# A four-layer trunk on one core: the sliding-window layer starts one query tile earlier, ends its gate tiles at head 12, and takes the sink as a key

## The chip, the cores and the metric

The kernel runs on one core of a Trainium2 chip. A core has TensorE (PE in the profile, its weight loads PEld), VectorE (DVE), ScalarE (ACT), GpSimd (POOL) and SyncE (SP, which here only issues transfers). The metric is the device time of one execution in microseconds (us); the kernel is run several times and the median counts.

## The reference

A trunk of four layers on x of 512 x 1024 (float32). Each layer is x + RMSNorm(branch(RMSNorm(x))), and each branch has an input projection, a mixer, a SiLU gate and an output projection. The mixers are a state-space layer, sliding-window attention, latent attention and a gated MLP. The change is in the second, for which the reference computes, with 16 heads of 64, two k/v heads, and a window of 128:

```python
q, k, v, z = jnp.split(h @ w_in, [SWA_WIDTH, SWA_WIDTH + kv_w, SWA_WIDTH + 2 * kv_w], axis=-1)
...
s = jnp.einsum('bnqhgd,bnkhd->bnhgqk', qb, kb).astype(jnp.float32) * (HEAD_DIM ** -0.5)
...
s = jnp.where(valid[None, :, None, None], s + bias, NEG_INF)
sink = jnp.broadcast_to(sinks.astype(jnp.float32).reshape(SWA_KV_HEADS, grp, 1, 1), s.shape[:-1] + (1,))
p = jax.nn.softmax(jnp.concatenate([s, sink], axis=-1), axis=-1)[..., :-1]
o = jnp.einsum('bnhgqk,bnkhd->bnqhgd', p.astype(v.dtype), vb)
...
return (o * jax.nn.silu(z)) @ w_out
```

The sink is one more logit of each softmax, without a value.

## The kernel before

Every dense product is done with operands split into a high part (fp32r) and a low part, three matmuls for one: high x high, low x high, high x low. XH and XL hold the layer's normalised input, transposed, and later, in the same memory, the gated output of the mixer, which the output projection reads.

**Weights** go through a list of chunks of 1 MB (`add`, L208). A chunk is loaded by SP into one of two buffers (`wraw`), copied to its high part `wh` by ACT, and its low part `wl` is the difference, made by POOL in one instruction of 128 x 2048 (L160), or, for chunks marked "mix", in four pieces alternating between POOL and DVE. `wh` and `wl` have two buffers each, and a third is kept for chunks marked "x". `get` (L191) hands out the next chunk; `ahead(n)` (L199) issues the splits of the next n chunks and the load of the one behind.

**Order.** A planner orders the instructions of each engine by priority and by its own estimate of when their inputs are ready, so what is issued first in the code can run later. Instructions issued through `act_`, `dve_`, `pool_`, `pe_`, or passed to `after`, keep their program order. On the chip every engine then runs its list in order. PSUM has eight banks, and every product takes one (`bank`).

**The sliding-window layer** (`layer_b`, L1360) does its input projection in tiles of 128 output features by 512 tokens, 24 matmuls each. The first four tiles (k, v, and query tiles 0 and 1) are done in two halves of 256 tokens: `fm_first` does the first half during the output projection of the layer before, `fm_rest` (L1289) the second half and then the copy out of PSUM. The fourteen other tiles come one by one from `Dense.step` (L1303): query tiles 2 to 7 and gate tiles z0 to z7. A query tile holds two heads; `evac_q` (L1378) copies its high part by ACT and subtracts its low part by DVE. v is turned by four transposes as soon as it is there, and the scores of head 0 are issued behind query tile 0.

For each head `scores(h)` (L1419) makes four blocks of scores on PE; DVE adds the bias, writes P and takes the row maximum in one instruction per block (L1433); `nm` is minus the larger of maximum and sink (L1439); ACT takes the exponential with its row sum, four instructions (L1444), and the sink's exponential `es` (L1446). `normalise(h)` adds `es` to the sums, takes the reciprocal and scales P on DVE (L1455). `p_transposes(h)` transposes P on PE, with the copies out split between DVE (L1473) and ACT (L1471). `pv(hp)` multiplies with v for a pair of heads and gates the result into `zt` (L1487). P has two buffers, so the scores of a head need the transposes two heads back. The loop over heads (L1494) issues the normalisation of head h, the scores of head h + 1, a dense tile, every second time a `pv`, and the transposes of head h. The last two gate tiles are done in halves, in heads 12, 13 (two), and 14.

`act_split(hp)` (L1489) splits a gated pair of heads from `zt` into XH and XL: ACT copies (L226), POOL or DVE subtracts (L227). XH and XL are the inputs of the dense tiles, so this may be written only after the last of them.

**The output projection** (`out_proj`, L290) has four blocks of 128 tokens, two column halves and two chunks of weights for each. It begins with the first chunk for all four blocks (12 matmuls each, into four banks that stay open), needing head pairs 0 to 3; the rest of the layer (`tail`: `pv(7)` and `act_split(7)`) is issued between them. All four layers use it.

Of the kernel before, what the change touches and what calls it, by code (L numbers as in the profile page):

```python
# [10 lines left out]
F32 = mybir.dt.float32  # L11
# [36 lines left out]
def tile_hybrid_trunk(ctx: ExitStack, tc: tile.TileContext, I, out, depth=4):  # L48
# [241 lines left out]
    def out_proj(SH, SL, x, begin, tail, emit_x, nxt, first):  # L290
# [9 lines left out]
        def mms(bt, t, i, HL, last, ks=range(4)):  # L300
            H, L = HL
            for k in ks:
                st, en = (i == 0 and k == 0), (last and k == 3)
                sh, sl = SH[:, t, 4 * i + k, :], SL[:, t, 4 * i + k, :]
                pe_.matmul(bt[:], lhsT=sh, rhs=H[:, k, :], start=st, stop=False)
                pe_.matmul(bt[:], lhsT=sh, rhs=L[:, k, :], start=False, stop=False)
                pe_.matmul(bt[:], lhsT=sl, rhs=H[:, k, :], start=False, stop=en)
# [1052 lines left out]
    def layer_b(tiles, reload):  # L1360
# [5 lines left out]
        sp.dma_start(out=sink[:], in_=dram("b_sinks", 0, [[0, 128], [1, 16]]))  # L1366
        bias = b1.tile([128, 16, 256], F32, name="bias")
# [21 lines left out]
        def evac(i, bt):  # L1389
# [29 lines left out]
        def scores(h):  # L1419
            g, q = h // 8, qs[h // 2][:, h % 2]  # L1420
            P = b1.tile([128, 4, 256], F32, name="P", bufs=2)
            mx = sb_.tile([128, 4], F32, name="mx")
            for pr in range(2):
# [6 lines left out]
                for n in (2 * pr, 2 * pr + 1):  # L1430
# [63 lines left out]
        for h in range(16):  # L1494
# [9 lines left out]
            elif 0 < h < 15:  # L1504
                dense.step()
# [517 lines left out]
```

## Time and profile before

| | |
|---|---|
| median of three runs | 1047.23 us (1045.99, 1047.23, 1049.91) |
| the profiled execution | 1044.97 us |
| its span, first to last instruction | 1043.2 us |
| mean granted clock of TensorE | 0.97 |
| busy: PE, PEld, DVE, ACT, POOL | 967.5, 798.5, 677.3, 488.1, 423.2 us |
| the sliding-window layer | about 305 to 475 us, its output projection behind it |

The profile gives for each engine the time that it executes instructions. A share of the whole span is an average over stages, so the views used here are taken by stretch of time: the busy time in a stretch with PEclk, the clock that TensorE was granted (1.00 is full); groups of instructions with their number, busy time and mean duration (ns), and the idle time of the engine before them with what ended it; waits, as "engine tile line <- what released it: us in total, times, longest"; and the timeline, with start and duration in us. Matmuls are pipelined, so a matmul's duration is longer than its distance to the next. An arrow reads out <- in.

### The profile page before, as it was taken

How to read it: one execution, taken by the hardware profiler on the slowest of the kernel's cores; microseconds unless marked ns; L12 is line 12 of the kernel's file. 1: busy time of each engine (PE TensorE's matmuls, PEld its weight loads, DVE VectorE, ACT ScalarE, POOL GpSimd, SP SyncE). 2: the span in 40 equal slices, each digit the busy share in tenths (PEclk: the TensorE clock that was granted, in tenths of full speed). 3: DMA queues.
4: the chain of work that ended last, by engine and by line, in shares of the span. 5: the costliest groups of instructions: out<-in, count | busy, mean ns of one | idle time of the engine just before them, and what ended most of it. 6: DMA issues, size and time to landing. Idle time of an engine off the chain costs nothing.

```text
span 1043.2 us, 14407 instructions
## 1 busy us (share of the span) xinstructions
PE 967.5 (93%) x5343; PEld 798.5 (77%) x5343; DVE 677.3 (65%) x1536; ACT 488.1 (47%) x1082; POOL 423.2 (41%) x325
## 2 busy tenths in 40 slices
PE   7879989999987999969899999999979999999997
PEld 6768988778777778757797877777747778888785
DVE  7998887735766867776840335878884876514454
ACT  4557776543456465562553252354463553322221
POOL 6775774666232122333436341312063433431210
PEclk8979999999998999989999999999999999999999
DMA  9211211454254132115034422110225032233011
GB/s 237 74 38 41 82 42 41 173 121 141 86 153 126 41 122 81 41 41 161 1 112 127 121 63 68 46 46 4 79 81 178 27 119 83 84 118 106 26 66 65
DMA packets 69223, 90.40 MB, mean 87 GB/s; under 512 B 13592, under 2 KB 49312, under 8 KB 69024
## 3 DMA queue, kind: packets, MB, share of 16 engines
q1 hardware_dynamic: 66944, 80.76, 25.2%
q10 hardware_dynamic: 2208, 8.72, 2.3%
q8 instruction: 42, 0.69, 0.3%
q14 instruction: 29, 0.24, 0.1%
HBM read 83.44 MB, written 4.98 MB: 85 GB/s over the span
## 4 chain that ended last, share of the span: by engine, by line
PE 62%; DVE 22%; ACT 9%; issue 4%; POOL 2%; DMA 0%; ACTq 0%; DVEq 0%; SPq 0%; POOLq 0%
PE bank L66 22%; PE bank L218 6%; PE bank L217 6%; PE bank L216 6%; PE bank L1792 4%; PE bank L1793 4%; PE bank L1794 4%; PE bank L101 2%; DVE rs_t L66 2%; DVE rs_y L66 2%; ACT P L1444 2%; PE bank L1685 2%; DVE xt L66 1%; PE bank L1729 1%; DVE P L1455 1%
## 5 line engine op out<-in xcount | busy, mean ns | idle before, releaser
L160 POOL TENSOR_TENSOR wl<-wraw,wh 128x2048 fp32r<-128x2048 f32 (+3 forms) x37 | 138.5, 3750 | 264.0 <-ACT wh L156 263.2
L217 PE MATMUL bank<-XL,wh 128*128 128x512 f32 (+1 forms) x542 | 186.9, 345 | 7.7 <-DVE XL L66 7.0
L216 PE MATMUL bank<-XH,wh 128*128 128x512 f32 (+1 forms) x542 | 188.6, 349 | 0.1
L218 PE MATMUL bank<-XH,wl 128*128 128x512 f32 (+1 forms) x542 | 186.6, 345 | 1.9 <-POOL wl L160 1.8
L66 POOL TENSOR_TENSOR wl<-wraw,wh 128x512 fp32r<-128x512 f32 (+1 forms) x63 | 90.1, 1454 | 104.0 <-ACT wh L66 90.5
L217 PEld LDWEIGHTS bank<-XL,wh 128*128 128x128 f32 x542 | 104.7, 193 | 20.6 <-DVE XL L66 7.7
L218 PEld LDWEIGHTS bank<-XH,wl 128*128 128x128 f32 x542 | 104.5, 193 | 14.7 <-POOL wl L160 2.2
L216 PEld LDWEIGHTS bank<-XH,wh 128*128 128x128 f32 x542 | 104.6, 193 | 12.6 <-ACT XH L1614 0.5
L66 PE MATMUL bank<-wh,XH 128*128 128x512 f32 (+1 forms) x320 | 112.6, 365 | 0.9 <-ACT g L66 0.9
L66 PE MATMUL bank<-wh,XL 128*128 128x512 f32 (+1 forms) x320 | 109.6, 355 | 0.0
L66 PE MATMUL bank<-wl,XH 128*128 128x512 f32 (+1 forms) x320 | 109.6, 355 | 0.0
L156 ACT CAST wh<-wraw 128x2048 fp32r<-128x2048 f32 (+3 forms) x50 | 71.0, 1439 | 45.8 <-PE bank L217 21.0
L1793 PE MATMUL bank<-wl,XH 128*128 128x512 f32 x192 | 76.3, 397 | 3.8 <-DVE wl L66 3.8
L66 DVE TENSOR_TENSOR wl<-wraw,wh 128x512 fp32r<-128x512 f32 x42 | 57.4, 1395 | 32.8 <-ACT wh L66 30.9
L1792 PE MATMUL bank<-wh,XH 128*128 128x512 f32 x192 | 76.8, 400 | 0.0
L1794 PE MATMUL bank<-wh,XL 128*128 128x512 f32 x192 | 76.3, 397 | 0.0
L66 PEld LDWEIGHTS bank<-wh,XH 128*128 128x128 f32 x320 | 60.3, 194 | 9.7 <-ACT g L66 1.1
L66 PEld LDWEIGHTS bank<-wh,XL 128*128 128x128 f32 x320 | 59.9, 193 | 9.1 <-DVE XL L66 0.2
L66 ACT CAST wh<-wraw 128x512 fp32r<-128x512 f32 (+1 forms) x105 | 59.4, 636 | 15.0 <-DMA wraw<-in_a_w_out_dram 7.6
L66 PEld LDWEIGHTS bank<-wl,XH 128*128 128x128 f32 x320 | 60.1, 194 | 8.2
L1694 ACT ACTIVATE P<-P,nm 128x512 f32<-128x512 f32 (+1 forms) x64 | 35.2, 550 | 53.4 <-DVE nm L1691 53.4
L1444 ACT ACTIVATE P<-P,nm 128x128 f32<-128x128 f32 (+1 forms) x64 | 30.1, 471 | 61.6 <-DVE nm L1439 61.6
(362 smaller groups left out, 2100.0 us busy)
## 6 DMA issues: line engine op xcount, KB each, us to landing
wraw<-in_d_w_in_dram SPq DMA_DIRECT2D x12, 1024.0 KB, 5.1
wraw<-in_b_w_in_dram SPq DMA_DIRECT2D x9, 1024.0 KB, 5.2
wraw<-in_c_w_in_dram SPq DMA_DIRECT2D x8, 1024.0 KB, 7.7
wraw<-in_a_w_in_dram SPq DMA_DIRECT2D x7, 1024.0 KB, 5.3
wraw<-in_c_w_uq_dram SPq DMA_DIRECT2D x8, 576.0 KB, 4.7
wraw<-in_a_w_glu_dram SPq DMA_DIRECT2D x4, 1024.0 KB, 5.1
wraw<-in_a_w_out_dram SPq DMA_DIRECT2D x4, 1024.0 KB, 5.0
wraw<-in_b_w_out_dram SPq DMA_DIRECT2D x4, 1024.0 KB, 4.9
```

The source lines that it names most:

```text
L66: return lambda *a, **k: after(f(*a, **k))
L101: pe.matmul(out_ap, lhsT=in_ap, rhs=ident[0:k, 0:k], is_transpose=True, start=True, stop=True)
L156: (act_ if c["eng"] in MIX else act).copy(h, r)
L160: es[(i + k) % len(es)].tensor_tensor(out=l, in0=r, in1=h.bitcast(F32), op=SUB)
L216: pe.matmul(out_ap, lhsT=lh, rhs=rh, start=(i == 0), stop=False)
L217: pe.matmul(out_ap, lhsT=lh, rhs=rl, start=False, stop=False)
L218: pe.matmul(out_ap, lhsT=ll, rhs=rh, start=False, stop=(i == n - 1))
L1444: act.activation(out=P[:, n, k0:256], in_=P[:, n, k0:256], func=AF.Exp, bias=nm[:, n:n + 1], accum_out=sums[:, n:n + 1])
L1694: act.activation(out=P[n][:], in_=P[n][:], func=AF.Exp, scale=scale, bias=nm[:, n:n + 1], accum_out=sums[:, n:n + 1])
L1792: pe.matmul(bt[:], lhsT=xh, rhs=H[:, k, :], start=(i == 0 and k == 0), stop=False)
L1793: pe.matmul(bt[:], lhsT=xh, rhs=L[:, k, :], start=False, stop=False)
L1794: pe.matmul(bt[:], lhsT=xl, rhs=H[:, k, :], start=False, stop=(i == 1 and k == 3))
```

## The change

Five things:

1. `layer_b` calls `ahead(1)` before `fm_rest`, so the split of the third weight chunk (query tiles 2 and 3) is issued ahead of the four first tiles.
2. The turning of v is a function of its own (`turn_v`). After `fm_rest` come one dense tile (query tile 2), then the turning of v, then the scores of head 0. All other dense tiles move up by one head, and the last, z7, is done whole in head 12; no tile is done in halves.
3. The sink becomes a 257th column of P. The scores are written negated, so DVE's reduction is a minimum that starts from minus the sink (a pointer scalar in place of a constant) and yields `nm` directly; ACT copies the sink's column into P (four elements a partition) and its exponentials run over 257 columns with scale -1. `nm`'s own instruction, `es` and the addition of `es` are gone.
4. The first chunk of the output projection is a class, `OutFirst`, of which `layer_b` calls `step` in heads 13, 14 and 15 (blocks 0, 1 and 2). `out_proj` does what steps are left: one in this layer, all four in the others, whose order stays the same.
5. The splits into XH and XL of head pairs 0 to 5 are issued in head 12 and of pair 6 in head 14, where before pairs 0 to 6 were issued in head 15. Pairs 0 to 3 and 7 are subtracted by DVE, 4 to 6 by POOL (before, odd pairs by DVE and even by POOL). In head 15 `ahead(2)` takes the place of `ahead(1)`, and `OutFirst` asks for one chunk ahead in this layer where `out_proj` asked for two. `tail` begins with `pv(7)`, behind all of the first chunk.

```diff
+    def out_mms(SH, SL, bt, t, i, HL, last, ks=range(4)):
...
+    class OutFirst:
+        def __init__(self, SH, SL, first):
+            self.S, self.first, self.bts = (SH, SL), first, []
+
+        def step(self):
+            t = len(self.bts)
+            if t == 0:
+                self.c0 = get()
+                ahead(self.first)
+            self.bts.append(bank())
+            out_mms(*self.S, self.bts[t], t, 0, self.c0, False)
+
-    def out_proj(SH, SL, x, begin, tail, emit_x, nxt, first):
+    def out_proj(pre, x, begin, tail, emit_x, nxt):
...
-        c0 = get()
-        ahead(first)
-        bts = []
-        for t in range(4):
-            bts.append(bank())
-            mms(bts[t], t, 0, c0, False)
+        while len(pre.bts) < 4:
+            pre.step()
             next(tail, None)
+        bts = pre.bts
...
+        nsink = b1.tile([128, 16], F32, name="nsink")
+        act.mul(nsink[:], sink[:], -1.0)
...
             elif i == 1:
                 act.copy(perm_out(vT[:]), perm_in(bt))
-                b2 = bank()
-                for n in range(4):
-                    transpose(b2[:, 128 * n:128 * n + 128], vT[:, 128 * n:128 * n + 128])
-                dve.tensor_copy(vs[:], b2[:].rearrange("p (n d) -> p n d", n=4))
             else:
                 evac_q(i - 2, bt)
-                if i == 2:
-                    scores(0)
+
+        def turn_v():
...
-            P = b1.tile([128, 4, 256], F32, name="P", bufs=2)
-            mx = sb_.tile([128, 4], F32, name="mx")
+            P = b1.tile([128, 4, 260], F32, name="P", bufs=2)
+            nm = sb_.tile([128, 4], F32, name="nm")
+            act.copy(P[:, :, 256:257], bc(bc(nsink[:, h:h + 1], 1, 4)[:, :, 0], 2, 1))
...
-                        out=P[:, n, k0:256], in0=sb[:, o0:o0 + 256 - k0], in1=bias[:, h, k0:256], scale=0.125,
-                        scalar=-3e38, op0=ADD, op1=MAX, accum_out=mx[:, n:n + 1])
+                        out=P[:, n, k0:256], in0=sb[:, o0:o0 + 256 - k0], in1=bias[:, h, k0:256], scale=-0.125,
+                        scalar=nsink[:, h:h + 1], op0=ADD, op1=ALU.min, accum_out=nm[:, n:n + 1])
...
-            nm = sb_.tile([128, 4], F32, name="nm")
-            dve.tensor_scalar(out=nm[:], in0=mx[:], scalar1=sink[:, h:h + 1], scalar2=-1.0, op0=MAX, op1=MUL)
             sums = sb_.tile([128, 4], F32, name="sums")
-            es = sb_.tile([128, 4], F32, name="es")
             for n in range(4):
                 k0 = 0 if n else 128
-                act.activation(out=P[:, n, k0:256], in_=P[:, n, k0:256], func=AF.Exp, bias=nm[:, n:n + 1],
+                act.activation(out=P[:, n, k0:257], in_=P[:, n, k0:257], func=AF.Exp, scale=-1.0, bias=nm[:, n:n + 1],
                                accum_out=sums[:, n:n + 1])
-            act.activation(out=es[:], in_=nm[:], func=AF.Exp, bias=sink[:, h:h + 1])
...
-            dve.tensor_tensor(out=sums[:], in0=sums[:], in1=es[:], op=ADD)
...
-                       dve if hp % 2 else pool)
-
+                       dve if hp < 4 or hp == 7 else pool)
+
+        ahead(1)
         fm_rest(tiles, evac)
+        dense.step()
+        turn_v()
+        scores(0)
         for h in range(16):
...
-            if h in (12, 13, 14):
-                for _ in range(2 if h == 13 else 1):
-                    dense.half()
-            elif 0 < h < 15:
+            if 0 < h < 13:
                 dense.step()
+            elif h >= 13:
+                pre.step()
             if h and h % 2 == 0:
                 pv(h // 2 - 1)
             if h == 6:
                 reload()
+            if h == 12:
+                for hp in range(6):
+                    act_split(hp)
+            if h == 14:
+                act_split(6)
             if h == 15:
-                ahead(1)
-                for hp in range(7):
-                    act_split(hp)
+                ahead(2)
             p_transposes(h)
 
         def tail():
-            yield
             pv(7)
             act_split(7)
+            B.close()
             yield
-            B.close()
         return tail()
```

More of the change, by code (lines that the diff above doesn't have):

```diff
@@ L288, in transpose_block @@
         x_low(bvs, t)
-    def out_proj(SH, SL, x, begin, tail, emit_x, nxt, first):
+    def out_mms(SH, SL, bt, t, i, HL, last, ks=range(4)):
+        H, L = HL
+        for k in ks:
+            st, en = (i == 0 and k == 0), (last and k == 3)
+            sh, sl = SH[:, t, 4 * i + k, :], SL[:, t, 4 * i + k, :]
+            pe_.matmul(bt[:], lhsT=sh, rhs=H[:, k, :], start=st, stop=False)
+            pe_.matmul(bt[:], lhsT=sh, rhs=L[:, k, :], start=False, stop=False)
+            pe_.matmul(bt[:], lhsT=sl, rhs=H[:, k, :], start=False, stop=en)
+    class OutFirst:
[9 more added lines that the diff above has]
+    def out_proj(pre, x, begin, tail, emit_x, nxt):
         ssq = [sm.tile([128, 2], F32, name="ssq") for t in range(4)]
@@ L298, in cs, with mms @@
             return slice(512 * n, 512 * n + 512)
[L300 to L307, printed above, removed]
+        def mms(*a):
+            out_mms(*pre.S, *a)
         def junk():
@@ L1358, in bias_lines, with layer_b @@
         sp.dma_start(out=scr, in_=bc(line[:], 1, 32))
-    def layer_b(tiles, reload):
+    def layer_b(tiles, pre, reload):
         B = ExitStack()
@@ L1399, in evac @@
                 act.copy(perm_out(vT[:]), perm_in(bt))
-                b2 = bank()
-                for n in range(4):
-                    transpose(b2[:, 128 * n:128 * n + 128], vT[:, 128 * n:128 * n + 128])
-                dve.tensor_copy(vs[:], b2[:].rearrange("p (n d) -> p n d", n=4))
             else:
                 evac_q(i - 2, bt)
-                if i == 2:
-                    scores(0)
+        def turn_v():
+            b2 = bank()
+            for n in range(4):
+                transpose(b2[:, 128 * n:128 * n + 128], vT[:, 128 * n:128 * n + 128])
+            dve.tensor_copy(vs[:], b2[:].rearrange("p (n d) -> p n d", n=4))
         def z_evac(kk):
@@ L1433, in scores @@
                     i = dve.tensor_tensor_reduce(
[L1434 to L1435 removed]
+                        out=P[:, n, k0:256], in0=sb[:, o0:o0 + 256 - k0], in1=bias[:, h, k0:256], scale=-0.125,
+                        scalar=nsink[:, h:h + 1], op0=ADD, op1=ALU.min, accum_out=nm[:, n:n + 1])
                     if h == 1:
                         after(i)
[L1438 to L1439 removed]
             sums = sb_.tile([128, 4], F32, name="sums")
[L1441 removed]
             for n in range(4):
                 k0 = 0 if n else 128
[L1444 removed]
+                act.activation(out=P[:, n, k0:257], in_=P[:, n, k0:257], func=AF.Exp, scale=-1.0, bias=nm[:, n:n + 1],
                                accum_out=sums[:, n:n + 1])
[L1446 to L1447 removed]
+            Ps[h], nms[h] = P, sums
         def normalise(h):
[L1450 to L1451 removed]
+            P, sums = Ps[h], nms.pop(h)
             dve.reciprocal(out=sums[:], in_=sums[:])
@@ L1509, in layer_b, with layer_c @@
                 reload()
+            if h == 12:
[3 more added lines that the diff above has]
+                act_split(6)
             if h == 15:
-                ahead(1)
-                for hp in range(7):
-                    act_split(hp)
+                ahead(2)
             p_transposes(h)
         def tail():
-            yield
             pv(7)
             act_split(7)
+            B.close()
             yield
-            B.close()
         return tail()
-    def layer_c(tiles, open_right, close):
+    def layer_c(tiles, pre, open_right, close):
         Cx = ExitStack()
@@ L1940, in tile_hybrid_trunk @@
     tail = iter(())
+    pre = OutFirst(YH, YL, 2)
     for l in range(depth):
@@ L1968, in tile_hybrid_trunk @@
             break
+        pre = OutFirst(XH, XL, 2 if l == 2 else 1)
         if l == 0:
-            tail = layer_b(tiles, lambda: after(sp.dma_start(
+            tail = layer_b(tiles, pre, lambda: after(sp.dma_start(
                 out=xt[:], in_=xd.rearrange("(b p) d -> p b d", p=128))))
@@ L1982, in close @@
                     right["loads"] = d_loads(pl)
-            tail = layer_c(tiles, open_right, close)
+            tail = layer_c(tiles, pre, open_right, close)
         else:
```

4 lines of the change are left out of this document (1 added, 3 removed).

## The prediction

> **What bounds the kernel now.** I read the page first, then the busy time by stretch around the sliding-window layer (it runs from about 305 to 481 us), then the waits of TensorE there, then the timeline at the two places where TensorE waits.
>
> ```profile
> span 1043.2 us, 14407 instructions
> ...
> PE 967.5 (93%) x5343; PEld 798.5 (77%) x5343; DVE 677.3 (65%) x1536; ACT 488.1 (47%) x1082; POOL 423.2 (41%) x325
> ```
>
> TensorE is busy 93% of the span, so time is to be had only where PE stands still or runs slow.
>
> ```profile
> core 0: us, PE busy (x) PEld busy (x) DVE busy (x) ACT busy (x) POOL busy (x), PEclk, DMA share, GB/s
> 306.30:347.70 41.40, 33.95 (x214) 30.72 (x212) 26.26 (x56) 24.77 (x48) 7.13 (x3) 0.92 0.43 102
> 347.70:434.20 86.50, 83.94 (x470) 67.01 (x469) 61.45 (x174) 47.80 (x112) 22.97 (x5) 1.00 0.25 86
> 434.20:480.90 46.70, 37.77 (x248) 31.18 (x247) 33.25 (x75) 23.28 (x58) 18.03 (x8) 0.93 0.23 70
> ```
>
> ```profile
> 319.00:323.00 4.00, 4.00 (x23) 4.00 (x23) 3.92 (x4) 3.61 (x4) 3.20 (x3) 0.58 0.03 7
> 329.00:333.00 4.00, 4.00 (x15) 3.33 (x14) 2.15 (x10) 1.75 (x7) 0.00 (x0) 0.57 1.01 340
> 457.00:462.00 5.00, 2.94 (x22) 1.93 (x22) 3.00 (x14) 3.46 (x12) 0.00 (x0) 1.00 0.00 0
> 466.00:470.00 4.00, 3.85 (x13) 3.29 (x14) 4.00 (x4) 2.90 (x6) 3.59 (x1) 0.61 0.01 4
> ```
>
> The middle of the layer (347.7 to 434.2) leaves PE idle 2.6 us of 86.5. The start leaves 41.40 - 33.95 = 7.45 us. The end, from the scores of head 13 to the last matmul of the output projection's first chunk, leaves 46.70 - 37.77 = 8.93 us. Both also have stretches of slow clock: 4 us at 0.58 and 4 us at 0.57 cost 1.7 us each against full speed, 3.85 busy us at 0.61 cost 1.5. So the start loses 7.45 + 3.4 = 10.9 us, the end 8.93 + 1.5 = 10.4 us, together 21.3.
>
> Who makes PE wait, first for 306 to 348, then for 434 to 481:
>
> ```profile
> PE bank L1428 <- DVE qS L1386: 3.6, 1, 3.6
> PE bank L101 <- issue: 2.1, 1, 2.1
> PE bank L101 <- DVE P L1455: 1.8, 1, 1.8
> ```
>
> ```profile
> PE bank L101 <- DVE P L1455: 5.5, 3, 3.0
> PE bank L1484 <- DVE PT L1473: 3.5, 2, 2.8
> ```
>
> At the start the scores of head 0 (L1428) wait 3.6 us for the low half of their query tile, and the transposes of v 2.1 us for the copy of v. At the end transposes of P wait for the normalised P (5.5) and P.V for the copied transposes (3.5).
>
> ```profile
> 321.67 4.57 POOL L160 TENSOR_TENSOR wl<-wraw,wh 128x2048 fp32r<-128x2048 f32 x1 [0.80 <-POOL wl L66]
> ```
>
> ```profile
> 322.01 5.38 DVE L66 TENSOR_TENSOR wl<-wraw,wh 128x512 fp32r<-128x512 f32 x2
> 327.43 2.17 DVE L1386 TENSOR_TENSOR qS<-bank,qS 64x512 fp32r<-64x512 f32 x2
> ```
>
> This is why the query tile is late: two weight splits on DVE (L66) start while POOL splits the next chunk, last 5.38 us together until POOL is done, and the query's subtraction queues behind them.
>
> **The change, part by part.** Tiles first: the chain has 140 wide matmuls in 31.86 us, 0.228 each, so a dense tile of 24 is 5.5 us and 12 matmuls of the output projection 2.7. Narrow ones follow each other at 0.12.
>
> ```profile
> 475.38 31.86 PE bank L66 x140
> ```
>
> ```profile
> 306.56 0.12 PE bank L216
> ```
>
> ```profile
> L1396 DVE TENSOR_TENSOR kL<-bank,kH 64x512 fp32r<-64x512 f32 x4 | 4.5, 1113 | 8.9 <-ACT kH L1393 8.9
> ```
>
> ```profile
> L1393 ACT CAST kH<-bank 64x512 fp32r<-64x512 f32 x4 | 4.3, 1082 | 3.7 <-PE bank L218 3.6
> ```
>
> 1. *The split of the third chunk moves ahead of the first four tiles.* Its four copies on ACT and four subtractions (two DVE, two POOL) move from behind k and v to before them; the load of a later chunk, which needs that raw buffer, moves with them past the bias loads on SP. ACT sits idle 3.6 us before the k copies and DVE 8.9 before k's low half; four copies of 0.62 and two subtractions of 0.68 undisturbed fit in. Cost nothing; if that cover were gone, about 2.5 us on the path k copies, k low, scores.
>
> 2. *One query tile before v is turned and before the first scores.* PE gets 5.5 us of work whose only input is step 1. The order of work becomes: k, v, q0, q1 (narrow, 24 x 0.12 = 2.8 each), the q tile, v turned, scores of head 0. One narrow tile still runs before k, so the q tile starts at about 306.5 + 5 x 2.8 = 320.5 and ends at 326. Without the weight splits in its way, the k chain takes its 4.3 (ACT) + 4.5 (DVE) from 312.3, the end of k's tile, to about 321, query tile 0 follows with 2.2 to about 323.5: 2.5 us before PE asks. The third wait (1.8) goes too, as head 0 is normalised behind a whole dense tile. What is late next is that 2.5 us margin, so I leave 1 us and take 10.9 - 1 = 9.9 us.
>
>    The trace says what a gap costs in clock: 2.1 us of waiting at 318 was followed by 4 us at 0.58, while the 2.8 us before 457 left 457 to 462 at 1.00. The Trainium skill, "TensorE: Matmul & The Clock Gate", Part 1, lets the clock fall after at least one idle window of about 3.4 us; by it the first gap would cost no clock and the start would be worth 1.7 us less. The 0.58 row contradicts it here, so I keep the row.
>
> 3. *The sink as a key.* Each head loses `nm` (L1439), the exponential `es` and the addition of `es`; it gains a 4-column copy on ACT. The score reductions take a pointer scalar instead of a constant.
>
> ```profile
> L1439 DVE TENSOR_SCALAR nm<-mx,sink x16: 224/230/2106, 331.0 to 458.3; 128x4 f32<-128x4 f32 x16
> L1446 ACT ACTIVATE es<-nm,sink x16: 281/282/285, 333.1 to 460.4; 128x4 f32<-128x4 f32 x16
> ```
>
> ```profile
> L66 DVE SCALAR_TENSOR_TENSOR zt<-zt,y x6: 677/678/1053, 202.0 to 205.4; 128x512 f32<-128x512 f32 x6
> L66 DVE SCALAR_TENSOR_TENSOR zt<-zt,rs_y,gpre x4: 744/748/751, 8.6 to 22.7; 128x512 f32<-128x512 f32 x4
> ```
>
>    Out of each head's loop go 0.23 (up to 2.1 where `nm` waited out POOL), 0.2 and 0.16. The new copy is bounded by the `es` row above (0.28, where its issue slot costs as much) and by zero, since it can run while ACT waits; I take it as equal to `es`. The pointer scalar's price on this reduction isn't in the trace: nearest is 748 against 678 ns, pointer against constant in another DVE form, +0.07; below is zero. Four per head make 0 to 0.28, I take 0.28. Net about 0.3 us off a loop that in the middle is covered by dense matmuls: worth 0 there, 2.6 at most (its idle time).
>
> 4. *z tiles end at head 12, the output projection's first 36 matmuls in heads 13 to 15.* PE's work is the same: one more dense tile early, 2.7 us in each of heads 13, 14, 15 instead of 2.7, 5.5 (head 13), 2.7, 0 from head 12 on. What they need is XH and XL of head pairs 0 to 3, which may be written only after z7's matmuls.
>
> ```profile
> L226 ACT CAST XH<-zt 128x512 fp32r<-128x512 f32 x8 | 4.6, 619 | 6.2 <-DVE zt L1487 6.2
> ```
>
> ```profile
> L227 DVE TENSOR_TENSOR XL<-zt,XH 128x512 fp32r<-128x512 f32 x4 | 7.1, 1786 | 0.7 <-ACT XH L226 0.7
> L1455 DVE TENSOR_SCALAR P<-P,sums 128x256 f32<-128x256 f32 x12 | 6.0, 555 | 0.0
> L1433 DVE CUSTOM_DVE_ANT_0 P<-bank,bias 128x256 f32<-128x256 f32 x12 | 4.5, 418 | 0.0
> ```
>
> ```profile
> DVE sums L1451 <- ACT es L1446: 8.3, 4, 2.2
> ```
>
> ```profile
> 473.72 1.67 PE bank L1484 x16
> ```
>
>    Behind z7 PE still has P.V (1.67), transposes (about 0.8) and scores (8 x 0.12 = 0.95): 3.4 us, against ACT's first copy at 0.62, each next one 0.62 later, and DVE's subtraction 0.68 behind it: four pairs by about 3.2. The projection's first matmuls just find them, if ACT takes the copies at once.
>    Then each head is a loop: exponentials 2.2 (the wait of L1451), reciprocal and normalisation about 1.5, copy of transposes 0.7, reductions 1.5: 5.9 us. PE's share per head is 2.7 + 0.95 + 0.8 + half of 1.67 = 5.3. So the loop is about 0.6 longer for three heads, 1.8 us, and the last transposes stand uncovered for about 1.2. DVE's extra four subtractions (2.7 us) fit in its 2.2 us waits per head, but POOL's 4.6 us split of the projection's second chunk now falls into heads 13 and 14 and can hold up a normalisation: 1.5. Residue 4.5; gain 10.4 - 4.5 = 5.9 us.
>
> 5. *Head pair 7 comes last.* P.V of pair 7 now follows the whole first chunk, where before 24 matmuls (5.5 us) came behind it.
>
> ```profile
> 475.43 0.69 DVE L1487 SCALAR_TENSOR_TENSOR zt<-bank,zt 128x512 f32<-128x512 f32 x1
> 476.81 0.69 DVE L227 TENSOR_TENSOR XL<-zt,XH 128x512 fp32r<-128x512 f32 x1 [0.69 <-ACT XH L226]
> ```
>
>    From the gate at 475.43, with ACT's copy (0.62) between, to the end of the subtraction at 477.50 it takes 2.1 us. The new cover is nine matmuls on pairs 4 to 6, 2.05 us, and two more on XH: cost 0 to 0.5, I take 0.5. The load of the post-norm gain starts at that event too and is now wanted after one tile instead of two; only DVE's gain multiply waits for it, and PE's next need of DVE is two column blocks later.
>
> Sum: 9.9 + 5.9 - 0.5 = 15.3 us. The profiled execution took 1044.97 (span 1043.2 and 1.8 around it), 2.3 below the median of the runs, 1047.23. So 1029.7 in the profiled execution's terms, 1032 against the median, which is the forecast.
>
> **Rivals.**
>
> *The end's hole only moves* (1037). The four subtractions at head 12 or a normalisation meet POOL, and the projection's matmuls stand at the head of PE's queue with transposes 13 and scores 15 behind them.
>
> ```profile
> 466.28 5.69 DVE L227 TENSOR_TENSOR XL<-zt,XH 128x512 fp32r<-128x512 f32 x2
> ```
>
> ```profile
> 466.41 5.01 POOL L160 TENSOR_TENSOR wl<-wraw,wh 128x2048 fp32r<-128x2048 f32 x1 [0.47 <-ACT wh L156]
> ```
>
> For it: two subtractions that take 0.69 alone took 5.69 beside POOL's 5.01. One such meeting costs 4.3 us, and a slow clock behind it 1.5: the end's 5.9 is gone, 1047.2 - 9.9 = 1037. The Trainium skill, "SBUF — State Buffer", SBUF: two separate sides, makes it a rule: the port pair shared by both is locked for a whole instruction; the trace agrees. Against: POOL's splits of pairs 4 and 5 come behind ACT's copies of 0 to 3. Chance 0.20.
>
> *The start comes out as before* (1041): the order of unpinned work is the planner's. For it: the trace has matmuls of q0 in front of v's transposes, which the code issues first.
>
> ```profile
> 315.50 0.28 PE L218 MATMUL bank<-XH,wl 128*128 128x256 f32 x1
> 317.86 0.63 PE L101 MATMUL bank<-ident,vT 128*128 128x128 f32 x4 [2.08 <-issue]
> ```
>
> If it pulls the next chunk's 4.6 us split in front of the query's subtraction, the wait of 3.6 stays, and with it the clock. Then only the end's gain is left, 5.9 or so. Chance 0.13.
>
> *Slower: DVE becomes the bound of each head* through the reduction with the pointer. In the middle DVE is busy 61.45 of 86.5 us over about ten heads: 2.5 us of slack per head, 0.6 for each of the four reductions. From 0.42 + 0.6 = 1.0 us on each head grows; it takes 0.25 more each (x 64 = 16 us) to eat the gain, so 1.3 us is the point. At 1.5 the kernel ends near 1032 + 64 x 0.5 = 1064. Nothing in the trace comes near: +0.07. Chance 0.07.
>
> *No difference*: both holes return elsewhere, at 1046. Chance 0.08.
>
> **How the numbers follow.** The forecast itself has the remaining 0.52, at 1032. The low end takes all 21.3 us of both ends and the 2.6 of the middle: 1047.2 - 23.9 = 1023. The high end takes in the first two rivals, to 1042. A measurement of this kernel tells about 0.5%, 5 us, from no change. Faster: 0.52 + 0.20 and two thirds of 0.13, 0.80; same: the rest of that and no difference, 0.13; slower 0.07.
>
> **What would show it.** Right: no wait of the first scores on the query's low half, clock 1.00 from 306 to 347, v's transposes behind a wide tile; the layer's matmuls of the output projection starting between the scores of heads 14 and 15; reductions at 0.42 to 0.50 us. Wrong: a wait of the projection's first matmul on XL, subtractions of 2 to 5 us at head 12, PE gaps over 2 us in heads 13 to 15, or the third chunk's split still behind the k copies.

## The result, and the profile after

The changed kernel took 1018.38 us (median of 1017.59 to 1019.33), the kernel before 1046.68 in the same comparison: a ratio of 0.9724, 95% interval 0.9701 to 0.9747. That is 28.3 us less, where 15.3 had been forecast, and below the low end of 1023. The profiled execution has a span of 1015.6 us. Times here and below leave out a few executions in a slower state, far above the others of the same kernel.

```profile
span 1015.6 us, 14293 instructions
...
PE 956.1 (94%) x5295; PEld 788.3 (78%) x5295; DVE 661.3 (65%) x1505; ACT 488.6 (48%) x1083; POOL 422.2 (42%) x324
```

The stretch of the layer, from the transposes of the last block before it to the end of the projection's first chunk with P.V of pair 7, by busy time: first before, then after.

```profile
306.56:480.90 174.34, 155.40 (x925) 128.65 (x924) 120.95 (x303) 95.60 (x217) 48.12 (x16) 0.96 0.29 86
```

```profile
307.84:454.80 146.96, 146.13 (x878) 121.21 (x876) 102.44 (x270) 95.79 (x217) 47.16 (x15) 1.00 0.31 95
```

It is 27.4 us shorter, nearly the whole gain. PE's idle time fell from 18.94 to 0.83 us, its clock from 0.96 to 1.00, and its *busy* time fell by 9.3 us for the same products. About 5 us of that is the slow clock, which the prediction had counted (3.4 + 1.5); the other 4 us or so were not traced. What PE still waits for between 305 and 456 us:

```profile
PE bank L101 <- DVE P L1469: 0.8, 1, 0.8
PE bank L66 <- ACT hblk L66: 0.6, 1, 0.6
```

In the chain of the last three heads the blocks of the output projection's first chunk (L66 x12) stand between transposes and scores, with no wait among them:

```profile
436.94 2.80 PE bank L66 x12
439.73 0.76 PE bank L101 x7
441.44 2.77 PE bank L66 x12
...
446.80 2.78 PE bank L66 x12
...
453.15 1.67 PE bank L1498 x16
```

The groups show one more thing: the idle time of ACT ahead of the exponentials, before (L1444) and after (L1460), fell from 61.6 to 27.1 us. It was the first sign that the key did more than had been forecast; it is not a measure of the gain, as the runs below show.

```profile
L1444 ACT ACTIVATE P<-P,nm 128x128 f32<-128x128 f32 (+1 forms) x64 | 30.1, 471 | 61.6 <-DVE nm L1439 61.6
```

```profile
L1460 ACT ACTIVATE P<-P,nm 128x129 f32<-128x129 f32 (+1 forms) x64 | 30.2, 475 | 27.1 <-DVE nm L1452 27.0
```

### The profile page after: what moved, and what is told of

It is laid out like the page before. It is cut to its first block, busy times and chain, and to the rows that moved or that the text cites. A ratio compares the mean times of both kernels' runs of the same rounds, so it can differ in the third digit from the quotient of the medians.

```text
span 1015.6 us, 14293 instructions
## 1 busy us (share of the span) xinstructions
PE 956.1 (94%) x5295; PEld 788.3 (78%) x5295; DVE 661.3 (65%) x1505; ACT 488.6 (48%) x1083; POOL 422.2 (42%) x324
## 4 chain that ended last, share of the span: by engine, by line
PE 68%; DVE 19%; ACT 5%; issue 4%; POOL 3%; DMA 0%; ACTq 0%; DVEq 0%; SPq 0%; POOLq 0%
PE bank L66 21%; PE bank L218 8%; PE bank L217 8%; PE bank L216 8%; PE bank L1811 4%; PE bank L1813 4%; PE bank L1812 4%; PE bank L101 3%; DVE rs_t L66 2%; DVE rs_y L66 2%; DVE xt L66 2%; PE bank L1704 2%; PE bank L1748 1%; PE bank L1498 1%; DVE P L1721 1%
## 5 line engine op out<-in xcount | busy, mean ns | idle before, releaser
L217 PE MATMUL bank<-XL,wh 128*128 128x512 f32 (+1 forms) x526 | 182.8, 347 | 7.7 <-DVE XL L66 7.0
L216 PE MATMUL bank<-XH,wh 128*128 128x512 f32 (+1 forms) x526 | 184.4, 352 | 0.1
L218 PE MATMUL bank<-XH,wl 128*128 128x512 f32 (+1 forms) x526 | 182.4, 347 | 1.8 <-POOL wl L160 1.8
L66 POOL TENSOR_TENSOR wl<-wraw,wh 128x512 fp32r<-128x512 f32 (+1 forms) x63 | 90.2, 1455 | 95.0 <-ACT wh L66 84.3
L217 PEld LDWEIGHTS bank<-XL,wh 128*128 128x128 f32 x526 | 100.5, 191 | 21.0 <-DVE XL L66 7.7
L218 PEld LDWEIGHTS bank<-XH,wl 128*128 128x128 f32 x526 | 100.4, 191 | 15.3 <-POOL wl L160 2.2
L66 PE MATMUL bank<-wh,XH 128*128 128x512 f32 (+1 forms) x320 | 111.2, 360 | 0.9 <-ACT g L66 0.9
L216 PEld LDWEIGHTS bank<-XH,wh 128*128 128x128 f32 x526 | 100.4, 191 | 13.1 <-ACT XH L1633 0.5
L66 PE MATMUL bank<-wl,XH 128*128 128x512 f32 (+1 forms) x320 | 108.8, 352 | 0.0
L66 PE MATMUL bank<-wh,XL 128*128 128x512 f32 (+1 forms) x320 | 108.5, 351 | 0.0
L66 DVE TENSOR_TENSOR wl<-wraw,wh 128x512 fp32r<-128x512 f32 x42 | 56.1, 1366 | 34.1 <-ACT wh L66 32.3
L66 PEld LDWEIGHTS bank<-wh,XH 128*128 128x128 f32 x320 | 59.1, 190 | 9.4 <-ACT g L66 1.1
L66 PEld LDWEIGHTS bank<-wh,XL 128*128 128x128 f32 x320 | 58.7, 189 | 9.0 <-DVE XL L66 0.2
L66 PEld LDWEIGHTS bank<-wl,XH 128*128 128x128 f32 x320 | 59.3, 191 | 8.0
L66 ACT CAST wh<-wraw 128x512 fp32r<-128x512 f32 (+1 forms) x105 | 59.4, 636 | 10.8 <-DMA wraw<-in_a_w_out_dram 7.9
L66 POOL TENSOR_TENSOR hblk<-xt,gpre 128x512 f32<-128x512 f32 x24 | 31.1, 1296 | 65.3 <-DVE xt L66 47.3
```

The costliest lines, as they stand in the source:

```text
L66: return lambda *a, **k: after(f(*a, **k))
L216: pe.matmul(out_ap, lhsT=lh, rhs=rh, start=(i == 0), stop=False)
L217: pe.matmul(out_ap, lhsT=lh, rhs=rl, start=False, stop=False)
L218: pe.matmul(out_ap, lhsT=ll, rhs=rh, start=False, stop=(i == n - 1))
```

## The experiments

**All combinations of three edits.** The change was taken apart into *start* (third chunk's split first, one query tile ahead of v's transposes and the first scores), *key* (sink as a key) and *end* (z tiles to head 12, first chunk in heads 13 to 15, its splits). Each was undone by putting the old lines back; where the counts of tiles did not fit, these lines differ from both kernels:

```diff
 # end without start: the fourteenth tile
-            if 0 < h < 13:
-                dense.step()
+            if 0 < h < 13:
+                for _ in range(2 if h == 12 else 1):
+                    dense.step()
 # start without end: thirteen tiles in the loop, z7 in halves
+            if h in (13, 14):
+                dense.half()
+            elif 0 < h < 12:
+                dense.step()
```

Start and end, without the key:

> The changed kernel with the old softmax (nm, es and the addition back, constant scalar in the reductions): start and end edits only. As predicted (the sink as a key is worth 0 in the middle, about 0.3 us a head in the last three): the changed kernel's 1018.4 plus 0 to 1, so 1018 to 1019.5. Rival, the key carries the middle: without it the 4.7 us that the middle gained beyond the forecast come back, 1023, PE waits on P L1469-like normalises or on nm between 345 and 434 us. Rival, the key also carries the end's surplus (7 us over 5.9 - 0.5): up to 1030.

Key and end, without the start:

> The changed kernel with the old start (v turned and scores 0 inside the first tiles, split of the third chunk behind them; the fourteenth dense tile runs at head 12 instead). As predicted: the start's 9.9 us come back and nothing else, 1028.3, with PE waits of about 3.6 on qS and 2.1 at the transposes of v. Rival, one tile more ahead of head 0 also carries the middle (DVE and ACT get a lead that lasts): 9.9 + 4.7, 1033.

Start and key, without the end:

> The changed kernel with the old end: 13 dense tiles are left for the heads, z6 whole at head 11, z7 as halves at heads 13 and 14, the four split pairs and the projection's first chunk behind head 15 as before. The tile that the start took comes out of the end, so its hole grows by up to 5.5 us: 1046.7 - 9.9 + 5.5 = 1042 if the end can't fill it, 1037 if the rest of the end is as before. If the key carries the middle: 4.7 less, 1033 to 1038.

The key alone:

> The kernel before with the sink as a key alone. As predicted: 0 in the middle and at most 2.6, 1044 to 1047; reductions 0.06 longer. Rival, the key shortens a loop that bounded the heads: 4.7 us in the middle and 2 in the last heads, 1040.

The end alone and the start alone, run later:

> The kernel before with the end edit alone (z tiles end at head 12, two of them there; out projection's first chunk in heads 13 to 15; head pair 7 last). My steps 4 and 5: 5.9 - 0.5 = 5.4 us less, 1042. If the head loop with the old softmax bounds the last heads (8 us lost there with start and end edits together): 1044 to 1047.

> The kernel before with the start edit alone (one query tile ahead of v's transposes and of the first scores; 13 dense tiles left, so the end has one half of z7 at heads 13 and 14 each). My step 2: 9.9 us less at the start, and up to 5.5 lost at the end, which has a tile less: 1037 to 1043. By the run with start and end edits (only 1.4 us gained at the start with the old softmax): no gain, 1044 to 1050.

Measured, with three distances read in the trace of one execution of each kernel: from the first copy of k (ACT, `kH`) to P.V of head pair 0 on PE; from there to P.V of pair 4; from there to the issue of the next layer's `rope` load. Where the start edit is in, one dense tile (5.5 us) has moved from the third stretch to the first; the table takes it out of the first and adds it to the third.

| edits | us | ratio to before, 95% | start | middle | end |
|---|---|---|---|---|---|
| none | 1046.7 | 1 | 42.1 | 68.8 | 109.8 |
| start | 1041.1 | 0.9929, 0.9912 to 0.9946 | 40.7 | 65.7 | 109.0 |
| end | 1040.2 | 0.9928, 0.9915 to 0.9941 | 41.7 | 68.8 | 103.7 |
| start, end | 1036.6 | 0.9891, 0.9878 to 0.9905 | 40.7 | 65.7 | 103.4 |
| key | 1032.2 | 0.9847, 0.9834 to 0.9860 | 39.9 | 67.4 | 95.8 |
| key, end | 1029.0 | 0.9817, 0.9801 to 0.9832 | 39.8 | 67.4 | 95.5 |
| start, key | 1024.1 | 0.9771, 0.9757 to 0.9784 | 31.4 | 65.6 | 99.2 |
| all (the change) | 1018.4 | 0.9724, 0.9701 to 0.9747 | 31.6 | 65.6 | 95.5 |

Here and below, differences are taken between ratios, times 1046.7, since each comparison had its own runs of the kernel before (by this measure the change gains 28.9). The key, which was priced at nothing, is the largest of the three: 16.0 us alone, 17.5 on top of the other two (0.9891 - 0.9724). All that was expected of the run without it (at most 1030), of the key alone (1040 at best) and of start and key (1033 at best) missed that. The run without the start came as expected, 1029.0 for 1028.3, with PE waiting 3.5 us for the query's low half and 2.0 before v's transposes. Alone the key shortens the end by 14.0 us; the end edit then adds 0.3, or 3.7 once the start has taken a tile away. The end edit alone gives 6.1 there. The start edit alone gains 1.4 at the start; on top of key and end, which have 2.3 there without it, it gains 8.2 more. The 1041 of the start edit alone falls in the range that step 2 gave, but by the middle, where the lead of one tile is worth 3.2.

**Why the key pays at the end.** DVE and ACT in one head, the kernel before:

```profile
448.77 0.28 DVE L1433 CUSTOM_DVE_ANT_0 P<-bank,bias 128x128 f32<-128x128 f32 x1
...
450.14 0.23 DVE L1439 TENSOR_SCALAR nm<-mx,sink 128x4 f32<-128x4 f32 x1
452.79 0.18 DVE L1452 RECIPROCAL sums<-sums 128x4 f32<-128x4 f32 x1
```

```profile
450.40 0.40 ACT L1444 ACTIVATE P<-P,nm 128x128 f32<-128x128 f32 x1 [3.89 <-DVE nm L1439]
```

and with the key alone:

```profile
438.95 0.33 DVE L1452 CUSTOM_DVE_ANT_0 P<-bank,bias,nsink 128x128 f32<-128x128 f32 x1
...
441.39 0.18 DVE L1466 RECIPROCAL sums<-sums 128x4 f32<-128x4 f32 x1 [0.89 <-ACT P L1460]
```

```profile
439.38 0.41 ACT L1460 ACTIVATE P<-P,nm 128x129 f32<-128x129 f32 x1 [1.11 <-DVE nm L1452]
```

Before, the first exponential starts 1.63 us after the first reduction: all four wait for one `nm` behind the fourth. With the key each waits for its own reduction, and the first starts after 0.43 us. From the first reduction to the reciprocal it takes 452.79 - 448.77 = 4.02 us before and 2.44 with the key: 1.2 less by the wait, 0.4 by the missing `es` and addition.

With the key alone PE waits for nothing from 434 to 482 us and its clock there is 1.00; before, it waited 5.5 + 3.5 us and ran at 0.53 and 0.61 from 462 to 470. The last two heads' normalisations also moved relative to POOL: before, three scalings took 1.80 us at 454.59 and 2.46 at 463.90, each beside POOL's subtractions (0.87 for three at 447.99, with POOL idle); with the key four take 1.08, at 441.61 and 449.07. How the 14.0 us split between the shorter wait and these meetings was not tested on the old end.

Two edits test the wait on the new one. One gives the change its wait back without an added instruction: the sink's column is written from all four minima.

```diff
-            act.copy(P[:, :, 256:257], bc(bc(nsink[:, h:h + 1], 1, 4)[:, :, 0], 2, 1))
 # behind the four reductions:
+            act.activation(out=P[:, :, 256:257], in_=nm[:].unsqueeze(2), func=AF.Identity, scale=0.0,
+                           bias=nsink[:, h:h + 1])
```

> The changed kernel with one edit: ACT's 4-column copy of the sink is written as 0 x nm + sink, so that it reads the row minima of all four blocks and stands ahead of the four exponentials. No instruction is added (the copy stays one ACT instruction of four columns). Theory A (the sink as a key pays because each block's exponential starts after its own reduction, while nm made all four wait for all four): most of what the old softmax cost comes back, 1018.4 plus 10 to 15, so 1028 to 1034, ACT waiting before each head's first exponential for the fourth reduction and PE for normalised P again. Rival B (it pays by the operations it removes, nm, es and the addition): 1018 to 1020, as all of them stay away.

Measured: 1023.5, ratio 0.9768 (0.9755 to 0.9780), 4.6 us more than the change: between A and B. A profile of it:

> The kernel with the restored wait (the sink's column written from all four minima) once more, for its trace: P.V of the first pair 37 us behind the first k copy as in the changed kernel (the start does not hang on the wait), and the 5 us that it lost in heads 13 to 15, where PE waits for normalised P.

P.V of pair 0 came 38.4 us behind the first k copy (37.1 in the change; the table has this less 5.5), and from P.V of pair 5 to that of pair 7 it took 23.4 us for 19.8: 1.3 lost at the start, 3.6 at the end. ACT's idle time ahead of the group is 42.2 us here. The other edit takes the wait out of the old softmax:

```diff
+                    dve.tensor_scalar(out=nm[:, n:n + 1], in0=mx[:, n:n + 1], scalar1=sink[:, h:h + 1], scalar2=-1.0,
+                                      op0=MAX, op1=MUL)
-            dve.tensor_scalar(out=nm[:], in0=mx[:], scalar1=sink[:, h:h + 1], scalar2=-1.0, op0=MAX, op1=MUL)
```

> Start and end edits with the old softmax (1036.6 when it ran), but nm computed for each block of its own, right behind that block's reduction: four DVE operations of one column for one of four. es and the addition stay. Theory A: the wait of all four exponentials for all four reductions is gone, so most of 17 us is gained, less 16 x (3 x 0.22 of nm, 0.2 of es, 0.17 of the addition) where DVE bounds a head: 1020 to 1026. Rival B: 48 more operations and none less: 1037 to 1042.

Measured: 1032.4, ratio 0.9850 (0.9833 to 0.9866), 4.3 less than with the old `nm`, with 48 operations more. P.V of pair 5 to pair 7 went from 27.8 to 23.1, the start only from 46.2 to 45.8. So the wait is worth 4 to 5 us, most of it in the last heads: theory A was right in kind and far too large. ACT's idle time ahead of the exponentials does not follow the time: it is 34.0 us here at 1032.4 and 26.5 with the key alone at 1032.2, against 27.1 in the change at 1018.4.

**Why the key pays at the start.** Start and end edits with the old softmax, PE's waits from 318 to 360 us and the busy time of ten of these:

```profile
PE bank L101 <- DVE P L1470: 6.9, 2, 5.7
```

```profile
337.00:347.00 10.00, 4.27 (x20) 3.34 (x19) 9.15 (x24) 5.05 (x12) 4.50 (x1) 0.79 0.16 42
```

DVE and POOL there:

```profile
335.93 0.81 DVE L1470 TENSOR_SCALAR P<-P,sums 128x128 f32<-128x128 f32 x3
337.70 2.19 DVE L1401 TENSOR_TENSOR qS<-bank,qS 64x512 fp32r<-64x512 f32 x2 [0.96 <-ACT qS L1398]
...
341.15 3.17 DVE L1470 TENSOR_SCALAR P<-P,sums 128x256 f32<-128x256 f32 x1
```

```profile
339.67 4.50 POOL L160 TENSOR_TENSOR wl<-wraw,wh 128x2048 fp32r<-128x2048 f32 x1 [15.29 <-ACT wh L156]
```

Three blocks of head 0 are normalised; the fourth is planned behind the query's subtraction and the next head's reductions, and lasts 3.17 us for some 0.3, until POOL's split ends (339.67 + 4.50 = 344.17). PE waits 5.7 us and then runs slow. In the change all four of head 0 go in one piece, ahead of POOL (head 1's four then take 2.30 us beside it, and PE waits the 0.8 shown above):

```profile
334.75 1.07 DVE L1469 TENSOR_SCALAR P<-P,sums 128x128 f32<-128x128 f32 x4
336.87 2.20 DVE L1403 TENSOR_TENSOR qS<-bank,qS 64x512 fp32r<-64x512 f32 x2 [1.05 <-ACT qS L1400]
```

The next edits keep that order with the old softmax, without and with `nm` by block:

```diff
             if h == 0:
+                normalise(0)          # its four scalings kept in program order
                 dense.step()
                 scores(1)
-            normalise(h)
+            else:
+                normalise(h)
```

> Start and end edits with the old softmax (1036.6), with head 0's normalisation written ahead of the next query tile and kept in that order: no operation is added or taken away. Without it DVE runs the fourth block of that normalisation behind the query's subtraction, where it meets POOL's split of a weight chunk and lasts 3.2 us for 0.29; PE waits 5.7 us and runs slow after it. Theory A2 (about 9 of the key's 17 us are this order at the start, the rest the end's loop): 1027 to 1029, P.V of the first pair 37 to 38 us behind the first k copy for 46.2. Rival (the start is lost by the length of the old softmax itself): 1034 to 1037.

> Both edits on the old softmax: head 0's normalisation kept ahead of the next query tile, and nm by block, so that each exponential follows its own reduction; es, the addition and four nm operations a head stay. Theory A2: the two gains add (9 at the start, 4 at the end), 1036.6 - 13 = 1023.5, the distance of some 4 to 5 to the changed kernel being the price of the operations that stay. If the operations cost nothing: 1019. If the order at the start is lost again: 1032.

The order alone gave 1032.7, ratio 0.9857 (0.9838 to 0.9877): 3.6 less, not 9. Its trace says why: head 0 is no longer late, but head 1's `nm` now meets POOL and lasts 2.56 us for 0.23, until POOL's end (339.58 + 4.61 = 344.19):

```profile
341.66 2.56 DVE L1454 TENSOR_SCALAR nm<-mx,sink 128x4 f32<-128x4 f32 x1
```

```profile
339.58 4.61 POOL L160 TENSOR_TENSOR wl<-wraw,wh 128x2048 fp32r<-128x2048 f32 x1 [15.34 <-ACT wh L156]
```

Both edits together gave 1022.3, ratio 0.9767 (0.9743 to 0.9790): 13.0 less, where the two alone gave 3.6 and 4.3. P.V of pair 0 now comes 38.6 us behind the first k copy, for 46.2 with neither, 44.2 with the order and 45.8 with `nm` by block. The second edit does two things, though. It also makes `nm` one column wide, and beside POOL's split these operations are not held, as head 1's of four columns was:

```profile
341.55 0.21 DVE L1454 TENSOR_SCALAR nm<-mx,sink 128x1 f32<-128x1 f32 x1
```

```profile
339.80 4.63 POOL L160 TENSOR_TENSOR wl<-wraw,wh 128x2048 fp32r<-128x2048 f32 x1 [14.62 <-ACT wh L156]
```

None of the 64 took more than 0.24 us. That fits a gain larger than the sum of the two, and it means that `nm` by block does not measure the joint wait alone; the edit on the sink's column does. So 13.0 of the key's 17.5 us are had without a sink column, by taking away ways in which a small operation is late.

**What the removed operations cost.** `es` and an addition put back into the change:

```diff
+            act.activation(out=es[:], in_=nm[:], func=AF.Exp, bias=sink[:, h:h + 1])
...
+            dve.scalar_tensor_tensor(out=sums[:], in0=es[:], scalar=0.0, in1=sums[:], op0=MUL, op1=ADD)
```

> The changed kernel with two operations of the old softmax put back where they hold up nothing but what they follow: the exponential es on ACT behind the four exponentials, and one DVE operation of four columns that adds 0 x es to the sums ahead of the reciprocal; no nm, each exponential still follows its own reduction. Predicted by my step 3 (0.2 + 0.16 us a head, covered in the middle): 1018.4 to 1019.5. Theory now (the 4 us between the old softmax with both waits broken, 1022.3, and the change are these operations): 1021 to 1023.

Both expectations missed: 1031.1, ratio 0.9842 (0.9830 to 0.9855), 12.4 us for some 0.36 us of operations a head. The start had the late fourth block again, and in head 13 three scalings, about 0.3 us each where POOL is idle, lasted 6.25 beside it, while ACT's idle time ahead of the exponentials was 26.3 us, no more than in the change:

```profile
340.93 2.92 DVE L1472 TENSOR_SCALAR P<-P,sums 128x256 f32<-128x256 f32 x1
...
438.74 6.25 DVE L1472 TENSOR_SCALAR P<-P,sums 128x256 f32<-128x256 f32 x3
```

```profile
438.43 1.54 POOL L227 TENSOR_TENSOR XL<-zt,XH 128x512 fp32r<-128x512 f32 x1 [10.11 <-ACT XH L226]
440.23 4.62 POOL L160 TENSOR_TENSOR wl<-wraw,wh 128x2048 fp32r<-128x2048 f32 x1 [0.27 <-ACT wh L156]
```

So the last test takes nothing away but the length of POOL's instruction: the layer's chunks are split in four pieces.

```diff
-                pool.tensor_tensor(out=l, in0=r, in1=h.bitcast(F32), op=SUB)
+            for i in range(4):
+                k = slice(i * n, i * n + n)
+                pool.tensor_tensor(out=l[:, k], in0=r[:, k], in1=h[:, k].bitcast(F32), op=SUB)
```

> The changed kernel with es and the addition put back (1031.1), with the same four pieces on POOL. There normalisations beside POOL's one instruction last 2.9 at the start and 6.3 us in head 13. Theory (the 12.7 us that two small operations cost are such meetings): most comes back, 1021 to 1025. Rival (the operations themselves, or the order): 1030 to 1032.

> Start and end edits with the old softmax (1036.6), but POOL makes the low half of this layer's weight chunks (input projection, and the first ones of the output projection) in four instructions of 128 x 512 for one of 128 x 2048: the same work, in pieces that end every 1.2 us. DVE's order at the start stays (the fourth block of head 0's normalisation behind the query's subtraction and a head's reductions). Theory (the start's loss is DVE shut out until POOL's instruction ends): the normalisation that lasted 3.2 lasts at most 1.5, PE's wait of 5.7 falls to some 4, and the last heads' meetings shrink too: 1029 to 1034. Rival (the loss is the order alone, or the length of the old softmax): 1035.5 to 1038.

With `es` and the addition: 1023.0, ratio 0.9748 (0.9728 to 0.9768): 9.8 of the 12.4 us came back, and the rest is within the intervals. The change itself was not run with the four pieces, so part of the 9.8 could be a gain that it would have too; the two groups above did get shorter, in the same places:

```profile
341.52 0.90 DVE L1480 TENSOR_SCALAR P<-P,sums 128x256 f32<-128x256 f32 x1
...
435.98 2.94 DVE L1480 TENSOR_SCALAR P<-P,sums 128x256 f32<-128x256 f32 x3
```

With the old softmax: 1035.2, ratio 0.9874 (0.9852 to 0.9895), no measurable gain over 0.9891, nearest its rival. The fourth block there lasted 1.16 us for 3.17, but `nm` behind it took 1.23 and PE still waited 3.7: the split into pieces makes each meeting shorter there, but not the order right. That the rest is the longer loop of the next head is likely and was not shown.

**The engine of the low halves**, the prediction's rival:

```diff
-                       dve if hp < 4 or hp == 7 else pool)
+                       dve if hp % 2 else pool)
```

> The changed kernel with the old choice of engine for the low halves: pairs 1, 3, 5 and 7 on DVE, 0, 2, 4 and 6 on POOL (in the change 0 to 3 and 7 on DVE). The rival of the prediction, one meeting of DVE and POOL on the shared port: a DVE normalisation or subtraction of 0.3 to 0.7 us lasts up to 4 or 5, and with the slow clock behind it the time rises by 4 to 6, 1022 to 1024. If the heads have that much slack: 1018 to 1019.5.

> The kernel with pairs 0 and 2 on POOL and 1 and 3 on DVE once more, for its trace: which operation of DVE beside POOL's subtractions or its chunk split lasts longer than alone in heads 12 to 15, and where PE waits for the 5 us that it lost.

Measured: 1023.7, ratio 0.9763 (0.9748 to 0.9778), some 4 us more than the change, the size that was expected, though its interval only just clears the change's and one execution took 1020.7. Its later profiled execution took 1019.4, with a layer 1.7 us longer (194.3 for 192.6 from the first k copy to the `rope` load) and a wait of 1.0 before a P.V. Whether a meeting cost the 4 us in the other executions stays open.

**The same idea in layer C.** Its causal attention has the same `nm`, and in the changed kernel it lasts up to 3.47 us, until POOL's end at 749.13:

```profile
745.69 3.47 DVE L1710 TENSOR_SCALAR nm<-mx 128x4 f32<-128x4 f32 x1
```

```profile
744.62 4.51 POOL L160 TENSOR_TENSOR wl<-wraw,wh 128x2048 fp32r<-128x2048 f32 x1
```

```diff
-  ... scale=1.0, scalar=-3e38, op0=ADD, op1=MAX, accum_out=mx[:, n:n + 1])
-            dve.tensor_scalar(out=nm[:], in0=mx[:], scalar1=-scale, scalar2=None, op0=MUL)
+  ... scale=-scale, scalar=3e38, op0=ADD, op1=ALU.min, accum_out=nm[:, n:n + 1])
-  ... func=AF.Exp, scale=scale, bias=nm[:, n:n + 1],
+  ... func=AF.Exp, scale=-1.0, bias=nm[:, n:n + 1],
```

> The changed kernel, with the same idea in layer C's causal attention: its reductions take scale -1/sqrt(96), minimum in place of maximum and write nm themselves, so the nm operation (L1710) goes and each block's exponential waits for its own reduction alone. Theory A: of layer C's PE waits on normalised P (7.3 us in the changed kernel) and of the slow clock after them (0.91 over 20 us, 0.88 over 28: 5 us) most goes: 1007 to 1012. Rival B: 16 operations of 0.2 to 0.3 us in a stage where PE has other work: 1015 to 1018.

Measured: 1007.8, ratio 0.9623 (0.9610 to 0.9635), 10.6 us less than the change and the fastest kernel of this study. PE's waits in layer C's heads, in the change and then without `nm`:

```profile
PE bank L101 <- DVE P L1721: 7.3, 7, 2.2
PE bank L218 <- POOL wl L160: 1.8, 2, 1.5
```

```profile
PE bank L101 <- DVE P L1719: 3.0, 3, 1.1
PE bank L1704 <- DVE nm L1707: 0.8, 1, 0.8
```

Beginning the projection's first chunk in layer C as well did not help:

```diff
+            if h >= 13:
+                pre.step()
-  ... zt[:, hp, :].rearrange("p (j c) -> p j c", j=4), pool)
+  ... zt[:, hp, :].rearrange("p (j c) -> p j c", j=4), dve if hp < 4 else pool)
```

> The changed kernel with layer C's nm gone (1007.8), and with the out projection's first chunk also begun in layer C: its blocks 0 and 1 in heads 13 and 14, low halves of pairs 0 to 3 on DVE in place of POOL. PE waits 1.1 + 0.8 us and runs at 0.91 for 20 us in that end (about 4 us lost). Theory: 2 to 4 us less, 1004 to 1006. Rival: a normalisation of layer C's end still meets POOL (5.9 us for two of 0.3 in the run before), and the hole only moves: 1007 to 1009.

1014.0, ratio 0.9681 (0.9661 to 0.9702), 6 us slower than without it. Two chunk splits now run back to back on POOL, two normalisations wait out both, and PE waits 6.0 us for a low half behind them:

```profile
730.40 9.13 DVE L1719 TENSOR_SCALAR P<-P,sums 128x384 f32<-128x384 f32 x2
```

```profile
730.13 9.12 POOL L160 TENSOR_TENSOR wl<-wraw,wh 128x2048 fp32r<-128x2048 f32 x2 [17.98 <-ACT wh L156]
```

## Why the prediction was wrong, step by step

The direction was right; the size failed at **step 3**. It summed the durations of the removed operations (0.3 us a head) and called them covered, worth 0 and 2.6 at most. Measured, the key alone is worth 16.0 us. Two things were left out. The key changes what waits for what: four exponentials no longer wait for four reductions, which with the missing operations shortens the way from first reduction to reciprocal by 1.6 us, not 0.3. Giving that wait back costs 4.6 us. And it removes operations whose place in DVE's list decides whether a normalisation or `nm` meets POOL's split; most of the key's 17.5 us on top of start and end goes with this, as 13.0 are had by the order and by `nm` in single columns, and two small operations put back cost 12.4. Signs of both stood in rows before: all of ACT's idle time ahead of the exponentials ended by `nm`, and the maximum of `nm` of 2106 ns, which was quoted. Neither gives the price. The prices asked for were right: the pointer scalar costs 0.06 us on a reduction (a median of 479 ns for 418; with a minimum and a constant, as in layer C without its `nm`, the same shape takes 420), against 0.07, and the copy 0.2, within its bounds:

```profile
L1452 DVE CUSTOM_DVE_ANT_0 P<-bank,bias,nsink x64: 336/479/502, 332.1 to 443.6; 128x256 f32<-128x256 f32 x48, 128x128 f32<-128x128 f32 x16
L1441 ACT COPY P<-nsink x16: 183/199/202, 318.8 to 440.9; 128x4 f32<-128x4 f32 x16
```

**Step 1** was right: the split ahead of k and v cost nothing that PE saw. **Step 2**: 9.9 predicted; on top of key and end the start edit brings 9.7, of which 8.2 in its stretch. The first two waits went as it says. "The third wait goes too" held only with the key, and there but for 0.8: without it that wait grew from 1.8 to 5.7, and the stretch gained 1.4. The step did not count on the key, so that its size came out is partly luck. **Step 4**: the end edit alone gave 6.1 us in its stretch, against 5.9 - 0.5, and 7.5 in all. In the change it comes on top of start and key and brings 4.9, 3.7 of it there, and the step's residue of 4.5 us is gone: that term rested on a loop of 5.9 us a head, summed as if exponentials and reductions followed each other. The trace has 4.5 a head on average from one block of the projection to the next (436.94 to 450.35 for three), with PE never idle. **Step 5** cost nothing for 0.5. Steps 2, 4 and 5 came to 15.3; start and end edits bring 11.4 without the key and 12.9 on top of it.

Of the **rivals**, the meeting of DVE and POOL cost the change's last heads nothing (two scalings of together 1.64 us, no wait of PE) and 0.8 us at its start, but it shows in most experiments; it stood in the prediction as a danger of the change, not as a loss of the kernel before. "The start comes out as before" is what the start edit alone did, by the planner's order as that rival said, though through the normalisation and not the query's subtraction. The reductions came nowhere near 1.3 us.

What stays open: the last 4.5 us between the old softmax with both repairs and the change, whose intervals just overlap. How much of it, if any, is the operations' own length and how much their place in the order was not settled; with POOL's pieces short, two of them put back cost 2.5 us, which the intervals do not tell from nothing.

## What to carry to other kernels

An operation's price is not its duration but the wait that it ends: before calling a few tenths covered, look at what one instruction makes a whole group wait for, here one four-column operation between four reductions and four exponentials, and let each block go by itself. Idle time ahead of a group, with one releaser for all of it, points to such a joint wait, but its length is no price: ACT's was 26 to 28 us in kernels of 1018 and of 1032 us. Look also for small operations that last far longer than their median beside another engine's long one. And where an engine's list is set by a planner, time an edit in combination: the same start edit gained 1.4 us at the start with the old softmax and 8.2 with the new, much of it by where one 0.3 us operation came to stand.

## What the hardware showed

How long DVE is shut out beside POOL was the surprise: every held operation shown in the experiments on POOL's uncut instruction ended within 0.3 us of POOL's, a four-column `nm` as much as a normalisation. Not everything was held: a one-column `nm` took 0.21 us beside POOL, and in the change a reciprocal of 128x4 took 0.18 at 341.57, as alone. Nor were reductions and copies that read PSUM: while POOL split from 339.67 to 344.17, three reductions took 0.42 us each, as ever, and with head 0's order kept a copy out of PSUM took 0.69 beside it. The Trainium skill, "SBUF — State Buffer", Who interferes with whom, bears on both: `copy`, `cast` and `tensor_scalar` can enter modes that need the pair of ports shared with GpSimd, where whoever issues first has the pair for its whole instruction and the other blocks, while a DVE instruction with at most one SBUF input outside such modes does not contend. The traces agree: the held scalings and `nm` are `tensor_scalar`, and the reductions read one operand from PSUM. With POOL's instruction cut in four, the group of three scalings took 2.94 us in place of 6.25.
